# A four-FFN encoder step on one core: loads behind the norm, the convolution's end on VectorE, one tag for each pair of banks

## The chip, the cores and the metric

One core of a Trainium2 chip runs the whole step. The metric is the device time in us, the median of several runs. The profile is one more execution on the same kind of core, recorded by the hardware profiler.

## What is computed

544 tokens (512 of a new stream, 32 that continue a cached one) with 1024 features go through two layers. Each layer is half an FFN, a mixer, and half an FFN; the mixer of the first layer is a convolution module, that of the second is differential attention. Cut to what matters here:

```
x = x + 0.5 * swiglu(rms_norm(x), w_gate, w_up, w_down)      # FFN0
a = rms_norm(x) @ w_pw1 + b_pw1                              # convolution module
u = a[..., :1024] * sigmoid(a[..., 1024:])
c = depthwise_conv(concat(past, u), w_dw, width 31, causal) + b_dw
c = silu(layer_norm(c) * ln_g + ln_b)
x = x + c @ w_pw2 + b_pw2
x = x + 0.5 * swiglu(...)                                    # FFN1
x = x + 0.5 * swiglu(...)                                    # FFN2
x = x + diff_attention(rms_norm(x))
x = x + 0.5 * swiglu(...)                                    # FFN3, then the last norm
```

All of it is float32.

## The kernel before

**Layout.** x lies in eight tiles of 128 features by 544 tokens. A matrix product in float32 is made of three TensorE (PE) products of rounded halves: weight high by data high, high by low, low by high. So every weight stripe (tile wr, ws or wd) is rounded on ScalarE (ACT) into whi (line L313), and the rest wlo is formed on VectorE (DVE) (L123, the helper `two`) before PE may use it; the data have xh and xl likewise. PE works in the tiles pq, py and pd of the FFNs and in a of the convolution, all in PSUM.

**FFNs and loads.** `ffns` opens an FFN and `ffn_body` walks through a plan of jobs; `task(n, f)` puts a piece of work in front of job n. Weights come by SyncE's (SP's) queue through `load(ring)` (L258): ring wr holds whole stripes for gate and up, ws stripes that a GpSimd (POOL) DMA adds others onto (`add_stripe`), wd smaller pieces of both products. `DEPTH` is 3 ws and 5 wd. On entry all of them are loaded (L534; the first FFN has a prologue in its place). Near the first job of the plan that needs the root (g1), `norm` (L667) sums the squares on PE, makes the reciprocal root r, and sends it through DRAM by SP (L484 row, L485 r) so that it is spread over all partitions; right behind it, still in `norm`, it fills the rings that are not full.

**Convolution.** `conv_body` (L754) has eight tiles of u. Four, called D, are convolved on DVE by 31 taps (L794), tap 0 and tap 1 on ACT (L790, L792), with two partial sums added at the end (L801). Four, called PT, are transposed by a trip through DRAM, convolved on PE (`pconv`, L892), written back from PSUM by ACT (L897), and sent out by an ACT DMA (dc, L899) and back by four SP DMAs (c, L902). The layer norm uses a shifted mean: the mean over the first D tile (`shift`, L930), tile mu, is taken from each tile (`center`, L914), the rest squared on ACT (`square`, L919), and both summed on PE (`sums`, L456). `keep_warm` (L467) is a number of matmuls of a constant whose result nobody reads. The statistics (L985 to L989) are broadcast by PE (`quarter_bcast`, L461), copied by ACT (L995), applied on DVE (L1014 to L1018) and ACT (L1021, L1022), and the last matrix product (pw2, `pw2_k`) follows, its lower half made by `y_lo` (L1007), its result added to x by `fin` (L1036).

The order of the work on an engine is the order in which these functions issue it. Eight PSUM banks are used as four pairs that go round, with one tag and four buffers:

```
conv(psum(4, [P, 2, 512], pp, "a", 4), V_F2)
```

Of the kernel before, what the change touches and what calls it, by code (L numbers as in the profile page):

```python
# [12 lines left out]
ALU = mybir.AluOpType  # L13
# [67 lines left out]
def trunk_kernel(ctx, tc, xT, ckT, cv, stT, stP, wtp, vec, gu0, dn0, pw1, pw2, gu1, dn1,  # L81
# [176 lines left out]
    def load(ring):  # L258
        i = nload[ring]
        if i >= (len(rings[ring]) if ring == "wr" else limit[ring]):  # L260
            return
        c = rings[ring][i]
        if ring == "wr":
            c["t"] = wraw.tile([P, WMAX], F32, tag="wr", name="wr")
        else:
            c["t"] = ffn_pool[0].tile([P, WMAX if ring == "ws" else QC], F32, tag=ring, name=ring, bufs=DEPTH[ring])
        nload[ring] += 1
        nc.sync.dma_start(out=c["t"][:, :c["n"]], in_=c["ap"])
        if ring == "ws":
            adding.append((pos["slot"], c))  # L270

    adding = []

# [244 lines left out]
    def product(out, w, off, kind, first, last, ks):  # L518
        hi, lo = w
        for i, k in enumerate(ks):  # L520
            a = off + i * P
            bh, bl = operand(kind, k)
            for z, (wt, b) in enumerate(((hi, bh), (hi, bl), (lo, bh))):
                nc.tensor.matmul(out=out, lhsT=wt[:, a:a + P], rhs=b, start=first and k == 0 and z == 0,  # L524
                                 stop=last and k == 3 and z == 2, skip_group_check=True)

    def ffns(plan, which, prologue=None):

        with tc.tile_pool(name="hp", reuse_waits="tile", bufs=1) as hp, \
             tc.tile_pool(name="pf", reuse_waits="tile", bufs=1, space=bass.MemoryType.PSUM) as pf:  # L530
            ffn_pool[0] = hp
            limit.update(plan["limit"])
            if prologue is None:
                for ring, n in DEPTH.items():  # L534
                    for _ in range(n):
                        load(ring)
            else:
                prologue()
            ffn_body(hp, pf, plan, which, prologue and "start")
            pos["get"] = plan["end"]  # L540

    def ffn_body(hp, pf, plan, which, entry):
# [124 lines left out]
        def norm():  # L667
            norm_a(ptile("y"), [nst["acc"]], AF.Silu)
            norm_c()
            for ring, n in DEPTH.items():  # L670
                while nload[ring] < n:
                    load(ring)

        for f in range(len(which)):
# [6 lines left out]
        for f in range(len(which)):  # L681
            g1 = at["Ga", f, 1, 0]
            start = entry and f == 0
            task(g1 - (1 if f else 0 if start else 2), norm)
            gc = which[f][0]
            sums_at = (-1, 0, 1, 4, 5) if start else (-2, -1, 0, 4, 5) if f else (None, None, None, -3, -2)
            for k, n in enumerate(sums_at):
                if n is not None:
                    task(g1 + n, lambda gc=gc, k=k: quarter_sums(k, gc), True)
            for k in range(KD // 2):  # L690
                task(g1 + (0 if f else 0 if start else 0), lambda k=k: quarter_minus(k), True)
                task(g1 + (3 if f else 3 if start else 3) + k, lambda gc=gc, k=k: quarter_diff(k, gc), True)
# [61 lines left out]
    def conv_body(alloc, next_gc, cp, dp):  # L754
        NO = UE - ST
        WTB = 6
        NFILL = (12, 8)
        WLN = {2: 2, 6: 3}
        taps = []
        u_t, c_t, x_t = {}, {}, {}  # L760
# [18 lines left out]
        def queue_taps(j):  # L779
            e = u_t[j]  # L780
            acc = []

            def tap(t):
                if t == 0:
                    acc.extend((ct(f"c{j}", [P, NO]), ct(f"d{j}", [P, NO])))
                    c_t[j] = acc[0]
                a = acc[t % 2]
                wcol = vcol(V_DW + j * CW + t)
                if t == 0:
                    nc.scalar.activation(out=a, in_=e[:, t:t + NO], func=AF.Identity, scale=wcol, bias=vcol(V_BDW + j))  # L790
                elif t == 1:
                    nc.scalar.activation(out=a, in_=e[:, t:t + NO], func=AF.Copy, scale=wcol)  # L792
                else:
                    nc.vector.scalar_tensor_tensor(out=a, in0=e[:, t:t + NO], scalar=wcol, in1=a,  # L794
                                                   op0=ALU.mult, op1=ALU.add)

            tap(0)
            tap(1)
            for t in range(2, CW):
                taps.append(lambda t=t: tap(t))  # L800
            taps.append(lambda: nc.vector.tensor_tensor(out=acc[0], in0=acc[0], in1=acc[1], op=ALU.add))  # L801

        def segs(j, dst):
            c = c_t[j]
            if j in D_T:
                return [(dst[:, 0:NPR], c[:, 0:NPR]), (dst[:, NPR:T], c[:, NPR + ST:NO])]
            out = []
            for d0, d1, n0, n1 in ((0, NPR, 0, 128), (NPR, T, 136, 144)):
                out.append((dst[:, d0:d1].rearrange("q (n p) -> q n p", p=4),
                            c[:, :, n0:n1].rearrange("q p n -> q n p")))  # L810
            return out

        trips = []
# [69 lines left out]
        def pconv(j):  # L883
            ps = alloc()
            xt = x_t.pop(j)
            cv_sb = ct("cvP", [P, 4, NU], bufs=2)
            b = 4 * P_T.index(j)
            for q in range(4):
                o = ps[:, q % 2, (q // 2) * 256:(q // 2) * 256 + NU]
                w = wt.pop(b + q)  # L890
                for t in range(NJ):
                    nc.tensor.matmul(out=o, lhsT=w[:, t * P:(t + 1) * P], rhs=xt[:, q, t:t + NU],  # L892
                                     start=t == 0, stop=t == NJ - 1)
                wt_load()
            for q in range(4):
                o = ps[:, q % 2, (q // 2) * 256:(q // 2) * 256 + NU]
                nc.scalar.activation(out=cv_sb[:, q, :], in_=o, func=AF.Identity, bias=vcol(V_BDX + 4 * j + q))  # L897
            d = dp.tile([4, 4, 32, NU], F32, tag="dc", name="dc", bufs=2)
            nc.scalar.dma_start(out=d.rearrange("g p c n -> (p c) g n"), in_=cv_sb)  # L899
            c = ct(f"c{j}", [P, 4, NU])  # L900
            for q in range(4):
                nc.sync.dma_start(out=c[32 * q:32 * q + 32], in_=d[q].rearrange("p c n -> c p n"))  # L902
            c_t[j] = c

        dtl = {}
        mu = ct("mu", [P, T])
        nbt = ct("nb", [P, T])

        sq_t = {}

        def center(j, eng):
            t = ct(f"d{j}", [P, T])
            for (o, i_), (m, _) in zip(segs(j, t), segs(j, mu)):
                eng.tensor_tensor(out=o, in0=i_, in1=m, op=ALU.subtract)  # L914
            dtl[j] = t

        def square(j):
# [7 lines left out]
        def shift():  # L925
            pm = alloc()
            c = c_t[D_T[0]]
            for o, src in ((pm[:, 0, 0:HT], c[:, 0:HT]), (pm[:, 1, 0:NPR - HT], c[:, HT:NPR]),
                           (pm[:, 1, NPR - HT:HT], c[:, NPR + ST:NO])):
                nc.tensor.matmul(out=o, lhsT=ones_m, rhs=src, start=True, stop=True)  # L930
            nc.scalar.activation(out=halves(mu), in_=pv(pm), func=AF.Copy)

        def taps_left(n):
            while len(taps) > n * (CW - 1):
# [3 lines left out]
        for j in range(KD):  # L938
# [3 lines left out]
            if j == 4:  # L942

                taps_left(3)
                shift()
                center(D[0], nc.gpsimd)
            elif j == 5:
                square(D[0])
            elif j == 6:
                pconv(PT[0])  # L950
                pop(10)
                taps_left(2)
                center(D[1], nc.gpsimd)
        trips_go()
        nc.scalar.preload_act_table(AF.Sqrt)
        square(D[1])
        pconv(PT[1])
        center(PT[0], nc.gpsimd)
        pop(12)
        pconv(PT[2])  # L960
        square(PT[0])
        pop(10)
        taps_left(1)
        center(D[2], nc.gpsimd)
        center(PT[1], nc.gpsimd)
        pop(4)
        pconv(PT[3])
        square(D[2])
        square(PT[1])
        pop(12)  # L970
        center(PT[2], nc.gpsimd)
        square(PT[2])
        pop(len(taps))
        center(D[3], nc.vector)
        square(D[3])
        pst = alloc()
        for n, j in enumerate((D[0], D[1], PT[0], D[2], PT[1], PT[2])):
            sums(j, n == 0)
        keep_warm(alloc(), NFILL[0])
        sums(D[3])  # L980
        center(PT[3], nc.vector)
        square(PT[3])
        sums(PT[3], last=True)
        rs4, nb4 = ct("rs4", [P, QT]), ct("nb4", [P, QT])
        nc.vector.tensor_copy(out=nb4, in_=pst[:, 0, 0:QT])  # L985
# [17 lines left out]
                mm3(pss[q], w2[0], (k % 2) * 4 + q, yh[k], yl[k], k == 0, k == KD - 1)  # L1003

        def y_lo(j):
            l = ct(f"c{j}", [P, T], F32R)
            nc.vector.tensor_tensor(out=l, in0=dtl[j], in1=f32(yh[j]), op=ALU.subtract)  # L1007
            yl.append(l)

        base = pos["get"]  # L1010
        for j in range(KD):
# [10 lines left out]
            nc.scalar.activation(out=t, in_=t, func=AF.Silu, scale=vcol(V_LNG + j), bias=vcol(V_LNB + j))  # L1022
            yh.append(h)
            if j == 0:
                pss = [alloc() for _ in range(4)]
            elif j in WLN:
                w_ahead(base + WLN[j])
# [13 lines left out]
        for o in range(4):  # L1041
            quarters(o, next_gc)
            flush(1)
            norm_sq(o)
        for o in range(4, KD):
            ps = alloc()
            w = w_get()
            for k in range(KD):
                mm3(ps, w, k, yh[k], yl[k], k == 0, k == KD - 1)
# [406 lines left out]
    with tc.manual_schedule():  # L1456
        nc.scalar.preload_act_table(AF.Sqrt)
        def prologue():
# [25 lines left out]
            for k in range(KD):  # L1484
                nc.sync.dma_start(out=x[k], in_=xT[:, k, :])
                for p in pieces.get(k, ()):
                    part(*p)
            load("wr")
            nc.sync.dma_start(out=vecs[:, V_HEAD:], in_=vec[:, V_HEAD:])
            nc.vector.tensor_scalar(out=ngain, in0=vecs[:, :V_FIN], scalar1=-1.0, scalar2=None, op0=ALU.mult)  # L1490
            for k in range(KD):
# [9 lines left out]
            for c in gates:  # L1501
                used(c)
                used(c)
            load("ws")
            nc.vector.tensor_tensor(out=lprod[:, 0:1], in0=vecs[0:64, V_LAM:V_LAM + 1],
                                    in1=vecs[0:64, V_LAM + 1:V_LAM + 2], op=ALU.mult)
            nc.vector.tensor_tensor(out=lprod[:, 1:2], in0=vecs[0:64, V_LAM + 2:V_LAM + 3],
# [119 lines left out]
```

## Time and profile before

| what | value |
|---|---|
| median of 3 runs | 2007.44 us (2006.48 to 2009.76) |
| the profiled execution | 2004.41 us, its span 2002.6 us |
| PE busy | 1956.4 us (98% of the span), 15548 matmuls |
| DVE, ACT, POOL busy | 1513.2, 977.9, 174.3 us |
| mean granted TensorE clock | 0.992 of full speed |

The rest of the execution's time lies outside the span. The convolution module is from about 400 to 600 us. The busy share of PE by 40 slices of the span (tenths) is 9 almost everywhere and drops in the first slice, in the eleventh (500 to 550 us) and in the last.

### The profile page before, as it was taken

What the parts mean: (1) busy time and instruction counts of PE and PEld (TensorE: products, weight loads), DVE (VectorE), ACT (ScalarE), POOL (GpSimd) and SP (SyncE); (2) the same over time, 40 slices, a digit from 0 to 9 for tenths busy, and PEclk for the clock granted to TensorE, in tenths of its full rate; (3) what the DMA queues carried; (4) which work ended last, traced back from release to release, by engine and by line L of the source; (5) the groups of instructions that cost most, each with busy time, mean ns of one, the idle gap of its engine ahead of it and who ended that gap; (6) DMA issues with size and microseconds to landing.
All of it is one profiled execution on the core that took longest, in us unless ns stands there. A gap on an engine that the chain in (4) does not pass through costs nothing.

```text
span 2002.6 us, 38720 instructions
## 1 busy us (share of the span) xinstructions
PE 1956.4 (98%) x15548; PEld 1922.0 (96%) x15548; DVE 1513.2 (76%) x2724; ACT 977.9 (49%) x1873; POOL 174.3 (9%) x209
## 2 busy tenths in 40 slices
PE   7999999999799999999999999999999999999998
PEld 6999999999699999999999999999888999999997
DVE  7877777699887877777787777776676678777775
ACT  6544444432265544444564444445555555444444
POOL 1000000013401000000000000000111000000000
PEclk9999999999899999999999999999999999999999
DMA  7655553236327655555155555322222256555522
GB/s 210 172 152 144 146 144 102 79 119 200 115 64 194 169 144 142 145 145 156 54 150 160 143 146 144 101 90 88 90 87 86 70 151 173 152 144 146 143 74 71
DMA packets 110787, 260.70 MB, mean 130 GB/s; under 512 B 11752, under 2 KB 23184, under 8 KB 110608
## 3 DMA queue, kind: packets, MB, share of 16 engines
q1 hardware_dynamic: 80528, 204.20, 30.6%
q0 software_dynamic: 25088, 50.69, 14.3%
q10 hardware_dynamic: 4992, 3.34, 0.5%
q8 instruction: 122, 2.00, 0.4%
q14 instruction: 57, 0.47, 0.1%
HBM read 248.87 MB, written 9.31 MB: 129 GB/s over the span
## 4 chain that ended last, share of the span: by engine, by line
PE 61%; DVE 6%; ACT 4%; issue 1%; DMA 1%; POOL 0%; DVEq 0%; ACTq 0%
PE pq L524 27%; PE pd L357 6%; PE pd L363 6%; PE pd L360 6%; PE py L524 4%; PE m L357 2%; PE m L363 2%; PE m L360 2%; DVE wlo L123 1%; ACT e L1167 1%; PE t L1180 1%; PE a L360 1%; PE t L1224 1%; PE a L363 1%; PE a L357 1%
## 5 line engine op out<-in xcount | busy, mean ns | idle before, releaser
L524 PE MATMUL pq<-ar,whi 128*128 128x272 f32 x1920 | 369.2, 289 | 3.2 <-ACT e L579 2.2
L524 PEld LDWEIGHTS pq<-ar,whi 128*128 128x128 f32 x1920 | 302.0, 189 | 4.3 <-ACT e L579 2.7
L123 DVE TENSOR_TENSOR wlo<-wr,whi 128x512 fp32r<-128x512 f32 (+1 forms) x243 | 196.1, 812 | 136.7 <-ACT whi L313 135.5
L524 PE MATMUL pq<-xh,whi 128*128 128x272 f32 x960 | 275.6, 287 | 3.0 <-DVE g L123 3.0
L524 PE MATMUL pq<-ar,wlo 128*128 128x272 f32 x960 | 277.6, 289 | 0.0
L524 PE MATMUL pq<-xh,wlo 128*128 128x272 f32 x960 | 276.5, 288 | 0.0
L524 PE MATMUL pq<-xl,whi 128*128 128x272 f32 x960 | 275.2, 287 | 0.0
L357 PE MATMUL pd<-hh,whi 128*128 128x272 f32 x1224 | 254.9, 289 | 0.2 <-DVE x L663 0.2
L360 PE MATMUL pd<-hl,whi 128*128 128x272 f32 x1224 | 252.8, 288 | 0.0
L363 PE MATMUL pd<-hh,wlo 128*128 128x272 f32 x1224 | 252.6, 288 | 0.0
L313 ACT ACTIVATE whi<-wd 128x512 fp32r<-128x512 f32 (+1 forms) x272 | 162.6, 599 | 162.8 <-issue 126.6
L278 POOL DMA_DIRECT2D ws<-gu x80 | 95.6, 1195 | 1261.8 <-DVE wlo L123 680.3
L123 DVE TENSOR_TENSOR wlo<-wd,whi 128x512 fp32r<-128x512 f32 (+1 forms) x272 | 177.3, 653 | 25.4 <-ACT whi L313 21.2
L357 PEld LDWEIGHTS pd<-hh,whi 128*128 128x128 f32 x1224 | 191.3, 188 | 1.3 <-PE py L363 0.4
L360 PEld LDWEIGHTS pd<-hl,whi 128*128 128x128 f32 x1224 | 192.3, 189 | 0.0
L363 PEld LDWEIGHTS pd<-hh,wlo 128*128 128x128 f32 x1224 | 191.7, 188 | 0.0
L524 PEld LDWEIGHTS pq<-xh,whi 128*128 128x128 f32 x960 | 180.8, 188 | 3.1 <-issue 3.1
L524 PEld LDWEIGHTS pq<-ar,wlo 128*128 128x128 f32 x960 | 181.7, 189 | 0.0
L524 PEld LDWEIGHTS pq<-xl,whi 128*128 128x128 f32 x960 | 180.8, 188 | 0.0
L524 PEld LDWEIGHTS pq<-xh,wlo 128*128 128x128 f32 x960 | 180.5, 188 | 0.1
L313 ACT ACTIVATE whi<-wr 128x512 fp32r<-128x512 f32 (+1 forms) x243 | 173.0, 717 | 15.3 <-PE pq L360 4.4
L663 DVE SCALAR_TENSOR_TENSOR x<-pd,x 128x544 f32<-128x544 f32 x168 | 121.0, 720 | 77.5 <-PE pd L363 77.4
(311 smaller groups left out, 4170.0 us busy)
## 6 DMA issues: line engine op xcount, KB each, us to landing
wr<-gu SPq DMA_DIRECT2D x94, 512.0 KB, 5.0
ws<-gu SPq DMA_DIRECT2D x80, 512.0 KB, 3.4
ws<-gu POOLq DMA_DIRECT2D x80, 512.0 KB, 6.8
wd<-dn SPq DMA_DIRECT2D x160, 256.0 KB, 2.8
wd<-gu SPq DMA_DIRECT2D x80, 256.0 KB, 2.7
wr<-pw SPq DMA_DIRECT2D x24, 512.0 KB, 3.3
wr<-qkv SPq DMA_DIRECT2D x24, 512.0 KB, 3.2
ar<-wtp SPq DMA_DIRECT2D x16, 576.0 KB, 4.8
```

Of the source, the lines that this page charges most:

```text
L123: nc.vector.tensor_tensor(out=out, in0=in0, in1=in1, op=op)
L278: nc.gpsimd.dma_start(out=c["t"].rearrange("p (a c) -> p a c", a=2), in_=c["add"], accum_op=ALU.add)
L313: nc.scalar.activation(out=hi, in_=src, func=AF.Copy)
L357: nc.tensor.matmul(out=o[s], lhsT=wh, rhs=xh[:, s * HT:(s + 1) * HT], start=first, stop=False)
L360: nc.tensor.matmul(out=o[s], lhsT=wh, rhs=xl[:, s * HT:(s + 1) * HT], start=False, stop=False)
L363: nc.tensor.matmul(out=o[s], lhsT=wl, rhs=xh[:, s * HT:(s + 1) * HT], start=False, stop=last)
L524: nc.tensor.matmul(out=out, lhsT=wt[:, a:a + P], rhs=b, start=first and k == 0 and z == 0, stop=last and k == 3 and z == 2, skip_group_che ...
L663: nc.vector.scalar_tensor_tensor(out=out, in0=src, scalar=0.5, in1=out, op0=ALU.mult, op1=ALU.add)
L1167: nc.scalar.activation(out=e[c][:, :n], in_=p, func=AF.Exp, bias=nm[:, c:c + 1], accum_out=sm[:, c:c + 1])
L1180: nc.tensor.matmul(out=p[c][:, :n], lhsT=d[a][pr, qs], rhs=d[b][pr, :n], start=z == 0, stop=z == 2)
L1224: nc.tensor.matmul(out=p[:, q], lhsT=a[:, ks], rhs=b[:, aq], start=(kb == 0 and z == 0), stop=(kb == 3 and z == 2))
```

## The change

**Loads.** An FFN's entry loads 2 ws and no wd; the rest (1 ws, 5 wd) is loaded by a task `fill` at job g1 + 2, behind the norm, in the first FFN of a plan. In the first FFN the two ws are issued before the tail of the constants and the wr of the prologue, where one ws followed the wr before. The DMA adds of ws are at least three jobs apart. **Convolution.** POOL has no centring any more: D0, D1 and the PT tiles are centred on DVE, the third and fourth D tiles have no centre at all, since their tap 1 moves from ACT to DVE and adds mu (held negated), and their closing addition writes 512 and 32 columns together. The PT tiles come back by quarters: four ACT copies each with its own 72 KB DMA out. The order of squares and sums changes, and a third filler group, five matmuls, is put ahead of pw2. **PSUM.** Four tags of one buffer each go round in place of one tag with four, and the last four pw2 rows take theirs ahead of the loop.

```
-            adding.append((pos["slot"], c))
+            adding.append((max(pos["slot"], adding[-1][0] + 3 if adding else 0), c))
...
+    opened = {"ws": 2, "wd": 0}
...
-                for ring, n in DEPTH.items():
+                for ring, n in opened.items():
...
+        def fill():
             for ring, n in DEPTH.items():
-                while nload[ring] < n:
+                while nload[ring] < first[ring] + n - (opened[ring] if not entry or ring == 'ws' else 0):
                     load(ring)
...
             task(g1 - (1 if f else 0 if start else 2), norm)
+            if not f:
+                task(g1 + 2, fill)
...
-        NFILL = (12, 8)
+        NFILL = (12, 8, 5)
...
+            late = j in D_T[2:]
...
+                elif t == 1 and late:
+                    nc.vector.scalar_tensor_tensor(out=a, in0=e[:, t:t + NO], scalar=wcol, in1=mu,
+                                                   op0=ALU.mult, op1=ALU.add)
...
+            def total():
+                c, d = acc
+                if not late:
+                    two(c, c, d, ALU.add)
+                    return
+                two(c[:, :NPR], c[:, :NPR], d[:, :NPR], ALU.add)
+                two(c[:, NPR:T], c[:, NPR + ST:NO], d[:, NPR + ST:NO], ALU.add)
+                dtl[j] = c[:, 0:T]
...
+            def back(q):
+                nc.scalar.activation(out=cv_sb[:, q, :], in_=bank(q), func=AF.Identity, bias=vcol(V_BDX + 4 * j + q))
+                nc.scalar.dma_start(out=d[q].rearrange("p c n -> (p c) n"), in_=cv_sb[:, q, :])
+                nc.sync.dma_start(out=c[32 * q:32 * q + 32], in_=d[q].rearrange("p c n -> c p n"))
...
-            nc.scalar.dma_start(out=d.rearrange("g p c n -> (p c) g n"), in_=cv_sb)
...
-        def center(j, eng):
+        def center(j):
             t = ct(f"d{j}", [P, T])
-            for (o, i_), (m, _) in zip(segs(j, t), segs(j, mu)):
-                eng.tensor_tensor(out=o, in0=i_, in1=m, op=ALU.subtract)
+            for o, i_, m in segs(j, t):
+                two(o, i_, m, ALU.add)
             dtl[j] = t
...
-        for n, j in enumerate((D[0], D[1], PT[0], D[2], PT[1], PT[2])):
+        for n, j in enumerate((D[0], D[1], PT[0], D[2], PT[1])):
             sums(j, n == 0)
         keep_warm(alloc(), NFILL[0])
+        sums(PT[2])
+        pop(len(taps))
+        square(D[3])
+        center(PT[3])
+        square(PT[3])
         sums(D[3])
-        center(PT[3], nc.vector)
-        square(PT[3])
         sums(PT[3], last=True)
...
+                keep_warm(alloc(), NFILL[2])
                 pss = [alloc() for _ in range(4)]
...
+        rows = [alloc() for _ in range(4)]
         for o in range(4, KD):
-            ps = alloc()
+            ps = rows[o - 4]
...
             load("wr")
+            for _ in range(2):
+                load("ws")
...
-            load("ws")
...
-            conv(psum(4, [P, 2, 512], pp, "a", 4), V_F2)
+            each = [psum(4, [P, 2, 512], pp, "a%d" % i, 1) for i in range(4)]
+            conv(lambda: (each.append(each.pop(0)), each[-1]())[1], V_F2)
```

How the order moves, at three places. On SP, behind the norm of the first FFN (row and r are the trip of the norm, wr, ws and wd the rings), first as it stood, then as it stands now:

```order
L484 DMA row<-r_347 4x136
L485 DMA r<-row 128x544
L268 DMA ws<-gu 128x1024 x2
L268 DMA wd<-gu 128x512
L268 DMA wd<-dn 128x256
L268 DMA wd<-gu 128x512
L268 DMA wd<-dn 128x256 x2
L268 DMA wr<-gu 128x1024 x2
```

```order
L484 DMA row<-r_349 4x136
L485 DMA r<-row 128x544
L268 DMA wr<-gu 128x1024 x2
L268 DMA ws<-gu 128x1024
L268 DMA wd<-gu 128x512
L268 DMA wd<-dn 128x256
L268 DMA wd<-gu 128x512
L268 DMA wd<-dn 128x256 x2
```

The two wr have moved in front of the ring's filling, and one ws of it has moved ahead of the row, into the prologue. On DVE, the end of the convolution (c and d the partial sums or centred tiles of a D tile, c_6206 and c_6173 the last PT tile in either program):

```order
L794 SCALAR_TENSOR_TENSOR c_5349<-u_5342,vecs,c_5349 128x574
L801 TENSOR_TENSOR c_5349<-c_5349,d_5350 128x574
L914 TENSOR_TENSOR d_6229<-c_5349,mu 128x512
L914 TENSOR_TENSOR d_6229<-c_5349,mu 128x32
L914 TENSOR_TENSOR d_6304<-c_6206,mu 128x512
L914 TENSOR_TENSOR d_6304<-c_6206,mu 128x32
```

```order
L806 SCALAR_TENSOR_TENSOR c_5349<-u_5342,vecs,c_5349 128x574
L123 TENSOR_TENSOR d_6236<-c_6098,mu 128x512
L123 TENSOR_TENSOR d_6236<-c_6098,mu 128x32
L123 TENSOR_TENSOR c_5349<-c_5349,d_5350 128x512
L123 TENSOR_TENSOR c_5349<-c_5349,d_5350 128x32
L123 TENSOR_TENSOR d_6307<-c_6173,mu 128x512
L123 TENSOR_TENSOR d_6307<-c_6173,mu 128x32
```

The centre of the third PT tile (d_6236) has come to DVE from POOL, and the one of the fourth D tile (d_6229) is gone. On PE, from the sums of the second PT tile to the broadcasts (d and c the centred tiles, u their squares, ones_m alone the fillers):

```order
L456 MATMUL a<-d_6155,ones_d 32x136 x4
L456 MATMUL a<-u_6213,ones_d 32x136 x4
L456 MATMUL a<-d_6224,ones_d 32x136 x4
L456 MATMUL a<-u_6227,ones_d 32x136 x4
L467 MATMUL a<-ones_m 128x128 x12
L456 MATMUL a<-d_6229,ones_d 32x136 x4
L456 MATMUL a<-u_6232,ones_d 32x136 x4
L456 MATMUL a<-d_6304,ones_d 32x136 x4
L456 MATMUL a<-u_6307,ones_d 32x136 x4
L467 MATMUL a<-ones_m 128x128 x8
```

```order
L456 MATMUL a_6241<-d_6163,ones_d 32x136 x4
L456 MATMUL a_6241<-u_6168,ones_d 32x136 x4
L467 MATMUL a_6282<-ones_m 128x128 x12
L456 MATMUL a_6241<-d_6236,ones_d 32x136 x4
L456 MATMUL a_6241<-u_6239,ones_d 32x136 x4
L456 MATMUL a_6241<-c_5349,ones_d 32x136 x4
L456 MATMUL a_6241<-u_6305,ones_d 32x136 x4
L456 MATMUL a_6241<-d_6307,ones_d 32x136 x4
L456 MATMUL a_6241<-u_6310,ones_d 32x136 x4
L467 MATMUL a_6339<-ones_m 128x128 x8
```

The twelve fillers stand one PT tile earlier, so that three pairs of sums follow them in place of two.

## Rows read from the trace of the kernel before

**Rows 1.** Waits of TensorE, whole span: us in total, times, longest us.

```profile
PE a L456 <- POOL d L914: 6.1, 3, 5.1
...
PE py L524 <- DVE g L123: 2.7, 2, 2.1
...
PE pq L357 <- DVE x L1036: 1.5, 1, 1.5
```

**Rows 2.** Windows: window, us, PE busy (x), PEclk, DMA share, GB/s.

```profile
41.00:47.00 6.00, 5.72 (x45) 1.00 0.56 102
...
50.00:54.00 4.00, 4.00 (x20) 0.57 0.09 13
...
541.00:548.00 7.00, 4.13 (x36) 1.00 0.01 2
...
549.00:556.00 7.00, 6.31 (x30) 0.55 0.00 1
```

**Rows 3.** Timeline of SyncE, first FFN: start, us, engine, line, op.

```profile
25.39 2.37 SPq L268 DMA_DIRECT2D ws<-gu  x2
...
30.70 3.33 SPq L268 DMA_DIRECT2D wr<-gu  x2
```

**Rows 4.** Timelines of ScalarE and VectorE, first FFN.

```profile
38.79 0.63 ACT L313 ACTIVATE whi<-wr 128x512 fp32r<-128x512 f32 x1 [3.37 <-DMA wr<-gu]
...
39.45 0.69 DVE L123 TENSOR_TENSOR wlo<-wr,whi 128x512 fp32r<-128x512 f32 x1 [4.08 <-ACT whi L313]
```

**Rows 5.** Timeline of TensorE, first FFN.

```profile
41.28 0.36 PE L524 MATMUL py<-xh,whi 128*128 128x272 f32 x1 [2.06 <-DVE g L123]
...
46.84 0.29 PE L524 MATMUL pq<-ar,wlo 128*128 128x272 f32 x1
...
49.88 0.40 PE L524 MATMUL pq<-ar,whi 128*128 128x272 f32 x1 [1.11 <-ACT e L579]
```

**Rows 6.** Timeline of VectorE, end of the convolution.

```profile
497.11 1.09 DVE L859 SCALAR_TENSOR_TENSOR u<-a,vecs,g 128x512 f32<-128x512 f32 x1
...
509.70 0.80 DVE L794 SCALAR_TENSOR_TENSOR c<-u,vecs,c 128x574 f32<-128x574 f32 x1
...
528.61 0.81 DVE L794 SCALAR_TENSOR_TENSOR c<-u,vecs,c 128x574 f32<-128x574 f32 x1
...
531.43 3.17 DVE L914 TENSOR_TENSOR d<-c,mu 128x512 f32<-128x512 f32 x4
...
556.30 0.72 DVE L1007 TENSOR_TENSOR c<-d,u 128x544 fp32r<-128x544 f32 x1
```

**Rows 7.** Timeline of GpSimd, end of the convolution.

```profile
515.36 19.19 POOL L914 TENSOR_TENSOR d<-c,mu 128x512 f32<-128x512 f32 x4 [5.49 <-DMA c<-dc]
```

**Rows 8.** Timelines of ScalarE and SyncE, end of the convolution.

```profile
524.11 0.37 ACTq L899 DMA_DIRECT2D dc<-cvP  x1
...
526.53 1.73 SPq L902 DMA_DIRECT2D c<-dc  x4
```

**Rows 9.** Timeline of TensorE, end of the convolution.

```profile
535.91 4.05 PE L467 MATMUL a<-ones_m 128*128 128x128 f32 x24
...
540.96 2.05 PE L467 MATMUL a<-ones_m 128*128 128x128 f32 x16
...
544.63 1.09 PE L461 MATMUL a<-nb,selq 128*128 128x136 f32 x8
...
548.06 0.52 PE L357 MATMUL a<-u,whi 128*128 128x272 f32 x2 [2.34 <-ACT u L1021]
...
549.69 0.82 PE L360 MATMUL a<-c,whi 128*128 128x272 f32 x2 [1.11 <-DVE c L1007]
```

**Rows 10.** DMA issues, whole span: xcount, KB each, median us to landing.

```profile
du<-u ACTq DMA_DIRECT2D x16, 72.0 KB, 4.2
...
dc<-cvP ACTq DMA_DIRECT2D x4, 288.0 KB, 6.0
...
c<-dc SPq DMA_DIRECT2D x16, 72.0 KB, 2.0
```

More of the change, by code (lines that the diff above doesn't have):

```diff
@@ L669, in norm @@
             norm_c()
+        first = {ring: nload[ring] for ring in DEPTH}
+        def fill():
             for ring, n in DEPTH.items():
-                while nload[ring] < n:
+                while nload[ring] < first[ring] + n - (opened[ring] if not entry or ring == 'ws' else 0):
                     load(ring)
@@ L795, in tap @@
                                                    op0=ALU.mult, op1=ALU.add)
+            def total():
[6 more added lines that the diff above has]
+                dtl[j] = c[:, 0:T]
             tap(0)
-            tap(1)
-            for t in range(2, CW):
+            if not late:
+                tap(1)
+            for t in range(1 if late else 2, CW):
                 taps.append(lambda t=t: tap(t))
-            taps.append(lambda: nc.vector.tensor_tensor(out=acc[0], in0=acc[0], in1=acc[1], op=ALU.add))
+            taps.append(total)
         def segs(j, dst):
@@ L805, in segs @@
             if j in D_T:
-                return [(dst[:, 0:NPR], c[:, 0:NPR]), (dst[:, NPR:T], c[:, NPR + ST:NO])]
+                return [(dst[:, 0:NPR], c[:, 0:NPR], mu[:, 0:NPR]), (dst[:, NPR:T], c[:, NPR + ST:NO], mu[:, NPR + ST:NO])]
             out = []
-            for d0, d1, n0, n1 in ((0, NPR, 0, 128), (NPR, T, 136, 144)):
+            for d0, d1, n0, n1, m0, m1 in ((0, NPR, 0, 128, 0, NPR), (NPR, T, 136, 144, NPR + ST, NO)):
                 out.append((dst[:, d0:d1].rearrange("q (n p) -> q n p", p=4),
-                            c[:, :, n0:n1].rearrange("q p n -> q n p")))
+                            c[:, :, n0:n1].rearrange("q p n -> q n p"),
+                            mu[:, m0:m1].rearrange("q (n p) -> q n p", p=4)))
             return out
@@ L887, in pconv, with bank @@
             b = 4 * P_T.index(j)
+            d = dp.tile([4, 4, 32, NU], F32, tag="dc", name="dc", bufs=2)
+            c = ct(f"c{j}", [P, 4, NU])
+            def bank(q):
+                return ps[:, q % 2, (q // 2) * 256:(q // 2) * 256 + NU]
+            def back(q):
+                nc.scalar.activation(out=cv_sb[:, q, :], in_=bank(q), func=AF.Identity, bias=vcol(V_BDX + 4 * j + q))
+                nc.scalar.dma_start(out=d[q].rearrange("p c n -> (p c) n"), in_=cv_sb[:, q, :])
+                nc.sync.dma_start(out=c[32 * q:32 * q + 32], in_=d[q].rearrange("p c n -> c p n"))
             for q in range(4):
-                o = ps[:, q % 2, (q // 2) * 256:(q // 2) * 256 + NU]
                 w = wt.pop(b + q)
                 for t in range(NJ):
-                    nc.tensor.matmul(out=o, lhsT=w[:, t * P:(t + 1) * P], rhs=xt[:, q, t:t + NU],
+                    nc.tensor.matmul(out=bank(q), lhsT=w[:, t * P:(t + 1) * P], rhs=xt[:, q, t:t + NU],
                                      start=t == 0, stop=t == NJ - 1)
@@ L895, in pconv @@
             for q in range(4):
-                o = ps[:, q % 2, (q // 2) * 256:(q // 2) * 256 + NU]
-                nc.scalar.activation(out=cv_sb[:, q, :], in_=o, func=AF.Identity, bias=vcol(V_BDX + 4 * j + q))
-            d = dp.tile([4, 4, 32, NU], F32, tag="dc", name="dc", bufs=2)
-            nc.scalar.dma_start(out=d.rearrange("g p c n -> (p c) g n"), in_=cv_sb)
-            c = ct(f"c{j}", [P, 4, NU])
-            for q in range(4):
-                nc.sync.dma_start(out=c[32 * q:32 * q + 32], in_=d[q].rearrange("p c n -> c p n"))
+                back(q)
             c_t[j] = c
         dtl = {}
-        mu = ct("mu", [P, T])
+        mu = ct("mu", [P, NO])
+        nc.gpsimd.memset(mu[:, NPR:NPR + ST], 0.0)
         nbt = ct("nb", [P, T])
         sq_t = {}
-        def center(j, eng):
+        def center(j):
             t = ct(f"d{j}", [P, T])
-            for (o, i_), (m, _) in zip(segs(j, t), segs(j, mu)):
-                eng.tensor_tensor(out=o, in0=i_, in1=m, op=ALU.subtract)
+            for o, i_, m in segs(j, t):
+                two(o, i_, m, ALU.add)
             dtl[j] = t
@@ L930, in shift @@
                 nc.tensor.matmul(out=o, lhsT=ones_m, rhs=src, start=True, stop=True)
-            nc.scalar.activation(out=halves(mu), in_=pv(pm), func=AF.Copy)
+            nc.scalar.activation(out=mu[:, 0:HT], in_=pm[:, 0, :HT], func=AF.Copy, scale=-1.0)
+            nc.scalar.activation(out=mu[:, HT:NPR], in_=pm[:, 1, 0:NPR - HT], func=AF.Copy, scale=-1.0)
+            nc.scalar.activation(out=mu[:, NPR + ST:NO], in_=pm[:, 1, NPR - HT:HT], func=AF.Copy, scale=-1.0)
         def taps_left(n):
@@ L945, in conv_body @@
                 shift()
-                center(D[0], nc.gpsimd)
+                center(D[0])
             elif j == 5:
@@ L952, in conv_body @@
                 taps_left(2)
-                center(D[1], nc.gpsimd)
+                center(D[1])
         trips_go()
@@ L957, in conv_body @@
         pconv(PT[1])
-        center(PT[0], nc.gpsimd)
+        center(PT[0])
         pop(12)
@@ L963, in conv_body @@
         taps_left(1)
[L964 to L967, printed above, removed]
+        center(PT[1])
         square(D[2])
         square(PT[1])
-        pop(12)
-        center(PT[2], nc.gpsimd)
+        pconv(PT[3])
+        pop(14)
+        center(PT[2])
         square(PT[2])
-        pop(len(taps))
-        center(D[3], nc.vector)
-        square(D[3])
         pst = alloc()
-        for n, j in enumerate((D[0], D[1], PT[0], D[2], PT[1], PT[2])):
+        for n, j in enumerate((D[0], D[1], PT[0], D[2], PT[1])):
             sums(j, n == 0)
         keep_warm(alloc(), NFILL[0])
+        sums(PT[2])
[3 more added lines that the diff above has]
+        square(PT[3])
         sums(D[3])
-        center(PT[3], nc.vector)
-        square(PT[3])
         sums(PT[3], last=True)
@@ L1005, in y_lo @@
         def y_lo(j):
-            l = ct(f"c{j}", [P, T], F32R)
+            l = ct(f"d{j}" if j in D_T[2:] else f"c{j}", [P, T], F32R)
             nc.vector.tensor_tensor(out=l, in0=dtl[j], in1=f32(yh[j]), op=ALU.subtract)
```

## The prediction

> **What bounds the kernel now.** I read the waits of the TensorE (PE) over the whole span first, because PE is the engine that hardly rests: an edit can only be worth something where PE stands still or runs at a low clock. Three entries of that view touch the change [rows 1]: 6.1 us for the centred tiles of the convolution (5.1 of it in one piece), 2.7 us in two pieces for VectorE's (DVE's) g at the entry of two FFNs, and 1.5 us for the last residual of the convolution. Then I read the clock that PE was granted, stretch by stretch [rows 2]: 1.00 (2.4 GHz) where PE was busy before, but 0.57 in 50 to 54 us and 0.55 in 549 to 556, which is near the lower of its two levels (1.2 GHz), each time just behind idle time of PE. Last I followed each wait back along the other engines' timelines [rows 3 to 8].
>
> **A. The start of the first FFN (loads).** The second load of the pair of wr stripes that SyncE (SP) issues behind the row r sits behind two ws and five wd loads: the ws are issued from 25.39 us, the wr from 30.70 [rows 3], the pair taking 3.33 us since the second waits. ACT then sits 3.37 us for a wr to land, and DVE 4.08 us for ACT [rows 4]; PE waits 2.06 for the g that is queued on DVE behind that split [rows 5]. The change issues those wr right behind r: 30.70 - 25.39 = 5.3 us earlier, more than the 4.08 us that DVE sits. The g comes forward by more than PE's wait, so A1 = **-2.06 us**. The work behind it (the split of the next stripes, ar, e) costs PE more: at the pitch of 5.72/45 = 0.127 us a matmul [rows 2], the one that starts at 46.84 is followed by five more of the same program order before 49.88 [rows 5]; six take 0.76 of the 3.04 us, and 2.28 are lost. It comes forward by 4.08 at DVE, but PE comes to it 2.06 earlier too, and I estimate that 0.99 of it stays (2.28 less 4.08 - 0.73 - 2.06, where 0.73 is the queue that DVE has to work off anyway, one pass of the size in [rows 4, 6]): A2 = **-1.29**. The clock of 50 to 54 was 0.57; at 1.00 the same columns take 4.00 x 0.43 = 1.7 us less. The wait of 2.06 at 41.28 alone left the clock at 1.00 behind it [rows 2, 5], so with one remaining gap of 1 us I take it as kept: A3 = **-1.7**, bounds 0 and -1.7. A's sum is **-5.05**. What pays: the two ws stripes and the five wd come later by the two wr, and the prologue now puts two ws ahead of the tail of the constants and two wr. No wait of PE in the view names a ws or a wd. The added GpSimd accumulates onto ws are spread by three slots, their number is unchanged. If they and the early ws take the wr's bandwidth by as much as the order gives it, A is 0; that is the other bound.
>
> **B. The end of the convolution.** GpSimd (POOL) stops centring. Before, its last four instructions span 19.19 us after waiting 5.49 for the tap data to come back [rows 7], while DVE works beside them; the four centring instructions that DVE runs there take 3.17 us [rows 6]. After, DVE does everything: u7 at the earliest 0.75 before its start at 497.11, that is 496.36 [rows 6]. From there the new order of DVE is u7, 5 taps, a centre of a tile convolved on PE (PT), 5 taps, the closing addition of the third DVE tile, 16 taps, PT centre, 14 taps, PT centre, closing addition, PT centre. A tap costs (528.61 - 509.70)/26 = 0.727 us [rows 6], a PT centre like u7's strided write 1.09 [rows 6] as the dearer bound, a closing addition 0.81 like a tap's whole time [rows 6]: 5 x 1.09 + 40 x 0.727 + 2 x 0.81 = 36.15, so the last centre ends near 532.5. Before, the last DVE instruction group ended at 531.43 + 3.17 = 534.60 [rows 6], and its sums stood still later: PE had 12 filler matmuls (24 passes) of 4.05 us queued at 535.91 ahead of them, at the low clock, and they ended at 540.96, where the next fillers start [rows 9]. In the new order the fillers come ahead of the sums of the third PT tile, so only a square on ACT (0.6 us, like the pass of [rows 4]) and two short groups of sums, under 1 us, follow the last centre: 534.0. B1 = 534.0 - 540.96 = **-7.0**. Bounds: if all that DVE does takes its bound without any loss and u7 starts early, -7.8; if the last PT tile comes back late, -5.8.
> That trip is the disputed piece. It goes out on ACT's queue and in on SP's. In the middle over the whole span one piece of 288 KB took 6.0 us out, pieces of 72 KB 4.2 on the same queue, and 2.0 each to come in [rows 10]. For this very tile the 288 KB went out at 524.11 and SP could begin to fetch it at 526.53, so it was out in 2.4 us [rows 8]. After, ACT copies and sends by quarters, 0.37 us more a quarter for the issue [rows 8], so the last quarter leaves near 524.11 + 4 x 0.37 = 525.6. With 2.4 and 2.0 it is in at 530.0, and DVE comes to it at 532.5 - 1.1 = 531.4: no wait, B1 stays -7.0. With 4.2 and 2.0 and half of the 1.73 us that SP takes for its four issues [rows 8] it is in at 532.6, 1.2 late: the -5.8. I take the row of this tile itself, since other loads are few there.
> The Trainium skill, DMA: Bandwidth & Descriptors, section Anatomy of one DMA, gives every DMA of the GpSimd path a fixed 2.0 us plus its bytes over a bandwidth, and so speaks against cutting one DMA into four: three more fixed costs. By that figure a quarter out takes an estimated 2.2 us, the last is in near 529.8, and the sum keeps its -7.0, unless the four fixed costs are paid one behind another, which is rival 3. The medians here, 4.2 and 6.0, lie above the page's figure, and by them the sum is -5.8.
> Then PE: the broadcasts ran at clock 1.00, behind 2.05 us of fillers [rows 2, 9]. The new sums come from a PE that has been idle longer, and the broadcasts may run at the low level: they are two of about 1.09 us at full clock [rows 9], so 0 to +2.1; I take B2 = **+0.5**, since most of the fillers that held the clock are still there. Behind the broadcasts PE waits 2.34 us for ACT's first u and 1.11 for DVE's c [rows 9] and then runs 549 to 556 at 0.55. That costs 7.0 x 0.45 = 3.15 us. The change puts five fillers into the first gap. Whether these suffice no row tells: 0 to -3.15; what is late next is DVE's third c, 556.30 + 0.72 = 557.02 [rows 6], which caps it. I take half, B3 = **-1.6**. B's sum is -7.0 + 0.5 - 1.6 = **-8.1**.
>
> **C. PSUM tags.** The first matmul of the FFN behind waits 1.5 us for the last residual [rows 1], because its buffer is the one that this row used. With tags and a filler tile more, the last row sits in another pair of banks and the first matmul asks for a row that was evicted several us earlier: **-1.5**. **D. The entries of the second and fourth FFN.** The r row is issued ahead of one ws and five wd loads; at the fourth, PE waited for g, the smaller of the two pieces, 2.7 - 2.1 = 0.6 to 0.7 [rows 1]: **-0.7**. At the second, the order of r changes under work that PE has anyway, so nothing.
>
> Sum: -5.05 - 8.1 - 1.5 - 0.7 = **-15.4 us**. The profiled execution was 2004.41 us, the median of the runs 2007.44, that is 3.03 above; the change gives 1989.0 in terms of the first and **1992.0** in terms of the second, which is the forecast.
>
> **The rivals.** (1) The start gains nothing: the early ws and the accumulates compete with the wr, which then land no sooner. A = 0, sum -10.3: 1997.1. For it: 5.3 us ahead in the queue is not 5.3 us ahead in landing, and the DMA share of 41 to 47 is still 0.56 [rows 2]. Against: the wr needs to come only 4.08 us earlier, and from 50 on the share is 0.09, so the loads before it are not more than the engines can carry. (2) The end of the convolution gains only part: the quarters make DVE wait (-5.8), the broadcasts run at the low clock (+2.1), and the five fillers don't lift it (0). B = -3.7, sum -11.0: 1996.5. Both together: -5.9, 2001.5. (3) Slower: the quarters out and in queue up behind one another. One trip was 6.0 + 2.0 = 8.0 us and ended where POOL went on at 515.36 [rows 7, 10]. Four in series take 32 us, 24 later: 539.4. DVE now meets that tile itself, in order, at 496.36 + 2 x 1.09 + 26 x 0.727 + 0.81 = 518.3, and all its taps queue behind the waiting centre, where before only POOL stood. It would stand 21.1 us; less the 15.4 won, that is 5.7 us slower: 2013.1. It decides from a slip of 518.3 - 515.36 + 15.4 = 18.3 us on. Against it: the pieces of 72 KB are sent in fours today too, and land in 4.2 us out and 2.0 in [rows 10]. (4) The change does not do what it says: PE's waits have other causes behind the ones named, so that the next of them ends at the same time; about 2007.
>
> **How the numbers follow.** The forecast has 0.58, the start alone failing 0.12, the end alone failing 0.14, both 0.06, no effect 0.06, slower 0.04. A difference of 0.2% (4 us, about what a measurement of this kernel can tell from none) is passed by the first three and by half of the fourth: faster 0.87, same 0.09, slower 0.04. The range goes from the forecast with B1 = -7.8, B2 = 0, B3 = -3.15 (1989.2) and 3 us of the runs' own spread below, 1986, up to both partial cases, 2001.5.
>
> **What would show it.** Right: DVE idles no 4.08 us before 40 us and PE's 2.06 there is gone; the clock of 50 to 54 us is near 1.00; no POOL work at the end of the convolution and no DVE tap over 1 us; the last sums at about 5 + 7 us earlier in the trace than 540.96, near 529 on its own axis; no wait of 1.5 at the hand-over. Wrong: DVE waiting for a quarter in the middle of its taps for over 2 us, a wait for wr, ws or wd in the first 60 us that was not there, or the matmuls behind the broadcasts still at 0.55.

## The result and the profile after

The changed kernel takes 1992.36 us (median of 6 runs, 1990.71 to 1993.75), the kernel before 2006.96 (6 runs, 2003.27 to 2009.76): a ratio of 0.9931, 95% interval 0.9921 to 0.9941, or 13.8 us. The profiled executions are 1992.63 and 2004.41 us, 11.8 apart, since that of before is one of its quicker ones.

The start of the first FFN, changed kernel: TensorE (PE), windows (window, us, PE busy, PEclk, DMA share, GB/s; PEclk is the granted clock as a share of 2.4 GHz), then ScalarE (ACT), GpSimd (POOL), SyncE (SP) and PE in their timelines (start, us).

```profile
35.00:41.00 6.00, 4.53 (x23) 0.56 0.77 211
41.00:47.00 6.00, 6.00 (x50) 1.00 0.20 37
50.00:54.00 4.00, 4.00 (x34) 1.00 0.39 130
```

```profile
26.19 1.16 ACT L313 ACTIVATE whi<-wr 128x512 fp32r<-128x512 f32 x2 [2.04 <-DMA wr<-gu]
...
16.88 2.55 POOL L278 DMA_DIRECT2D ws<-gu  x2 [14.09 <-DMA ws<-gu]
...
27.72 0.33 SPq L485 DMA_DIRECT2D r<-row  x1
28.15 0.89 SPq L268 DMA_DIRECT2D wr<-gu  x2
...
36.47 0.57 PE L524 MATMUL pq<-xh,whi 128*128 128x272 f32 x1 [5.03 <-DVE g L123]
```

The kernel before has a wait of 2.96 at that PE row, and the full clock in 35 to 41 us:

```profile
34.47 0.36 PE L524 MATMUL pq<-xh,whi 128*128 128x272 f32 x1 [2.96 <-DVE g L123]
...
35.00:41.00 6.00, 4.21 (x34) 1.00 1.09 332
```

The wait of 2.06 at 41.28 and the idle time up to 49.88 [rows 5] are gone and 50 to 54 us runs at 1.00 instead of 0.57 [rows 2]. But an earlier wait has grown from 2.96 to 5.03, and the clock is low behind that one (0.56 in 35 to 41).

The end of the convolution, changed kernel, VectorE (DVE) and PE:

```profile
494.95 1.19 DVE L883 SCALAR_TENSOR_TENSOR u<-a,vecs,g 128x512 f32<-128x512 f32 x2
...
529.78 1.20 DVE L123 TENSOR_TENSOR d<-c,mu 128x512 f32<-128x512 f32 x2
```

```profile
524.54 2.94 PE L467 MATMUL a<-ones_m 128*128 128x128 f32 x24
529.11 0.53 PE L456 MATMUL a<-d,ones_d 128*32 128x136 f32 x8 [1.62 <-DVE d L123]
...
532.15 2.05 PE L467 MATMUL a<-ones_m 128*128 128x128 f32 x16
```

Against [rows 9]: the twelve fillers (24 passes) take 2.94 us instead of 4.05 and are over at 527.5, before VectorE's last centre, and the sums end at 532.15 instead of 540.96. From u7 to the end of the last centre VectorE takes 529.78 + 1.20 - 494.95 = 36.03 us; no tap on VectorE is over 0.823 us (those into tile c are shown, those into d have the same maximum):

```profile
L806 DVE SCALAR_TENSOR_TENSOR c<-u,vecs,c x60: 801/808/823, 401.5 to 527.3; 128x574 f32<-128x574 f32 x60
```

### The profile page after: what moved, and what is told of

The parts are those of the page before. It is cut to its first block, busy times and chain, and to the rows that moved or that the text cites. A ratio compares the mean times of both kernels' runs of the same rounds, so it can differ in the third digit from the quotient of the medians.

```text
span 1990.8 us, 38773 instructions
## 1 busy us (share of the span) xinstructions
PE 1952.1 (98%) x15558; PEld 1920.8 (96%) x15558; DVE 1509.8 (76%) x2736; ACT 977.7 (49%) x1873; POOL 147.1 (7%) x198
## 4 chain that ended last, share of the span: by engine, by line
PE 86%; DVE 7%; ACT 4%; DMA 2%; issue 2%; SPq 0%; ACTq 0%; DVEq 0%
PE pq L524 36%; PE pd L357 8%; PE pd L363 8%; PE pd L360 8%; PE py L524 6%; PE a L357 2%; PE a L360 2%; PE a L363 2%; PE m L357 2%; PE m L363 2%; PE m L360 2%; DVE wlo L123 1%; PE pq L357 1%; PE a L926 1%; PE pq L360 1%
```

## The experiments

Every kernel's PE timeline was cut at the same points: the first product of the PT tiles behind the last product of pw1 (the convolution module's first matrix product), the first filler behind the last sums, the first pw2 product with c, and the first product of the next FFN with xl. The first column is the time at the first point, the next three are the stretches between the points, and the rest is from there to the end of the span. Each is one profiled execution; all in us. Every ratio below is to runs of the kernel before taken beside that kernel, whose medians lie between 2006.08 and 2007.96 us.

| kernel | PT products start | to sums' end | to first c | to next FFN | rest |
|---|---|---|---|---|---|
| before | 495.53 | 45.43 | 8.73 | 52.60 | 1400.31 |
| changed | 493.11 | 39.04 | 8.73 | 49.74 | 1400.18 |
| ws behind wr | 491.16 | 38.36 | 8.75 | 49.58 | 1401.15 |
| loads alone | 491.63 | 45.99 | 8.74 | 52.61 | 1399.83 |
| end alone | 497.33 | 39.09 | 8.74 | 51.40 | 1399.64 |
| fillers moved | 497.02 | 42.74 | 8.74 | 52.29 | 1399.81 |
| POOL centres | 493.98 | 40.69 | 8.97 | 49.74 | 1399.42 |
| no third fillers | 491.92 | 38.26 | 8.74 | 49.74 | 1400.54 |
| one dc | 494.28 | 38.38 | 8.74 | 49.57 | 1400.23 |
| rows in loop | 492.84 | 40.19 | 8.74 | 49.59 | 1401.74 |
| changed again | 492.51 | 38.38 | 8.74 | 49.57 | 1401.20 |
| together | 490.76 | 38.14 | 8.74 | 49.70 | 1399.66 |
| adds left out | 491.21 | 38.96 | 8.73 | 49.58 | 1399.32 |

**One part alone: the loads.** The hunks on `adding`, `opened`, `fill` and the prologue, on the kernel before.

> The kernel before with the loads' part alone (two ws and no wd at an entry, the rest behind the norm, the prologue's order, the adds spaced). Theory: it gives what the start of the changed kernel's trace shows, 2.4 us up to the convolution, plus 0.7 at the entry of the fourth FFN: about 3 us faster than before. Rival (the terms A and D of the prediction): 5.05 + 0.7 = 5.7 us faster.

2001.65 us, ratio 0.9976 (0.9964 to 0.9987): 4.8 us, between the two; the interval, 2.6 to 7.2 us, leaves room for both. The theory took the profiled execution of before for a usual one. Two kernels with the old loads (the next two) start the PT products at 497.33 and 497.02, not 495.53.

**One part alone: the convolution's end.** All hunks of `conv_body` but the rows taken ahead.

> The kernel before with the convolution's end alone (centring on VectorE, tap 1 with mu, quarters, order of sums and fillers, the third filler group); loads and PSUM tags as before. Theory: sums that end 6.4 us earlier and a clock that is low for 3 us less behind the broadcasts: 8.0 us faster than before, and 9.5 if the tile that the third filler group takes is what moves the last row to another pair of banks, so that the wait of 1.5 us at the hand-over goes without the tags. Rival (the gain of the end needs the earlier loads of the start): under 5 us.

1998.63 us, ratio 0.9955 (0.9940 to 0.9969): 9.0 us. The rival is out (the interval is 6.2 to 12.0 us). The theory holds, and the trace says in which form: the hand-over's wait stays, in spite of the filler tile (us in total, times, longest):

```profile
PE pq L357 <- DVE x L1058: 1.6, 1, 1.6
```

**The fillers alone**, on the kernel before:

```
-        for n, j in enumerate((D[0], D[1], PT[0], D[2], PT[1], PT[2])):
+        for n, j in enumerate((D[0], D[1], PT[0], D[2], PT[1])):
             sums(j, n == 0)
         keep_warm(alloc(), NFILL[0])
+        sums(PT[2])
```

> The kernel before with one edit: the sums of the third PT tile stand behind the twelve fillers instead of ahead of them. GpSimd still centres. Theory (the larger part of the gain at the convolution's end is that the fillers no longer stand between the last centres and their sums): the last sums end near 536.4 instead of 540.96, 4.5 us faster than before. Rival (GpSimd beside VectorE is what holds the end up): less than 1.5 us faster.

2002.86 us, ratio 0.9982 (0.9973 to 0.9992): 3.6 us (interval 1.6 to 5.4). In the table the sums end 2.7 us sooner, neither 4.5 nor under 1.5. The fillers now wait for GpSimd too, by the sums ahead of them:

```profile
532.37 1.40 PE L456 MATMUL a<-d,ones_d 128*32 128x136 f32 x8 [4.90 <-POOL d L914]
...
534.40 3.90 PE L467 MATMUL a<-ones_m 128*128 128x128 f32 x24
```

So the order alone gives 2.7 of the 45.43 - 39.04 = 6.4 us. The rest comes only with the other edits of the end: no centres on GpSimd, and two centres fewer.

**GpSimd's centres back** in the changed kernel (`center(D[0], nc.gpsimd)` and so on for D0, D1 and three PT tiles).

> The changed kernel with the centres of D0, D1 and the first three PT tiles back on GpSimd; the last PT tile stays on VectorE, D2 and D3 have no centre, order of sums and fillers as changed. Theory (GpSimd beside VectorE stretches both, and its last centre is late): a centre on GpSimd of up to 15 us again, sums that end 2 to 4 us later, so 2 to 4 us slower than the changed kernel (1994.5 to 1996.5). Rival (what was gained beyond the fillers' order is the two centres that are gone, and GpSimd hides the rest): within 1 us of the changed kernel.

Median 2000.6 us, ratio 0.9958 (0.9941 to 0.9975), but the seven runs lie between 1994.34 and 2004.64. That is 8 us above the changed kernel by the medians, 5.4 by the ratios, so the rival falls, and the 2 to 4 us of the theory are too few. The profiled run, 1994.58, is among the quick ones. Its sums end 1.65 us later than in the changed kernel, and PE waits for a GpSimd centre of 9.03 us, where the first centre on GpSimd, at 452.65, takes 2.03. VectorE is stretched too: four taps and a closing addition beside GpSimd's centres take 2.0 to 2.4 us instead of 0.8. So in this execution 4.7 of the 6.4 us stay with GpSimd centring; what makes other runs 6 to 10 us slower its trace doesn't show.

```profile
522.48 9.03 POOL L943 TENSOR_TENSOR d<-c,mu 128x512 f32<-128x512 f32 x2 [6.00 <-DMA c<-dc]
...
530.89 1.33 PE L456 MATMUL a<-d,ones_d 128*32 128x136 f32 x8 [4.92 <-POOL d L943]
...
L806 DVE SCALAR_TENSOR_TENSOR c<-u,vecs,c x60: 802/810/2424, 402.3 to 528.7; 128x574 f32<-128x574 f32 x60
```

**No third fillers** (the `keep_warm(alloc(), NFILL[2])` line out).

> The changed kernel without the third group of fillers (five matmuls behind the broadcasts). Theory (they shorten the stretch of low clock behind the broadcasts): TensorE's gap there is 2.3 us again, the clock stays low until some 6.5 us behind the first product instead of 4.3, 1.6 us slower than the changed kernel. Rival (VectorE's third c sets the pace there, or the fillers do nothing for the clock): within 0.5 us. A second difference is bound up with it: the tile they take is gone, so the last rows sit in another pair of banks and the wait of 1.6 us at the hand-over may be back; the trace tells the two apart.

1993.45 us, ratio 0.9930 (0.9915 to 0.9945). The time can't tell 0.5 from 1.6 us, but the stretch can: 49.74 to the next FFN, as with the fillers. The theory falls. The clock there is low for about 3 us, as in the changed kernel (0.83 and 0.60 in 540 to 543 and 543 to 546), and PE still is not late:

```profile
540.00:543.00 3.00, 3.00 (x16) 0.50 0.00 0
```

The kernel with the rows in the loop (below) has the full clock all through this stretch, and it is 49.59 there:

```profile
543.00:546.00 3.00, 3.00 (x26) 1.00 0.00 0
```

Where PE has the full clock in this stretch it waits for VectorE's third c, as in that kernel (1.10 at 549.16) and in the one with the ws behind the wr:

```profile
545.66 0.52 PE L360 MATMUL a<-d,whi 128*128 128x272 f32 x2 [1.08 <-DVE d L1036]
```

That c is the floor of 49.6 to 49.7 in the table: about 3 us at the low clock cost at most 0.2 us here.

**One transfer out for each PT tile** (`back` only copies; one ACT DMA behind the four).

> The changed kernel with one 288 KB transfer out for each PT tile again instead of four of 72 KB; the four transfers in as they are. Theory (VectorE comes to each centre later than either way of sending brings the tile): within 1 us of the changed kernel; the first centre behind u7 is the only one that could wait. Rival (the quarters are what lets VectorE take the centres without standing): VectorE waits 1 to 2 us at a centre and the sums end that much later.

1993.17 us, ratio 0.9928 (0.9913 to 0.9943). The theory holds: within 1 us of the changed kernel by median and ratio, and VectorE doesn't wait for a tile. The quarters are not what lets VectorE centre.

**The rows in the loop again** (`ps = alloc()` in place of `rows[o - 4]`).

> The changed kernel with the last four rows of pw2 allocated inside their loop again; four tags stay. Theory (the wait at the hand-over to the next FFN hangs on the tags, that is on which pair of banks the next pool's first tile waits for): no wait of 1.6 us comes back, within 0.5 us of the changed kernel. Rival (it hangs on the rows taken ahead): the wait is back, 1.5 us slower.

1993.12 us, ratio 0.9926 (0.9910 to 0.9943), within 1 us of the changed kernel; no hand-over wait. It is gone without the third fillers too, and it stands with the end alone (1.57) and with the loads alone (1.56), so this leaves the tags as its cure. In this trace one quarter did come late, the last. SyncE's fetches of four earlier quarters took 4.28 us (3.10 in the changed kernel), and the ar of the PT products behind them in its queue were issued at 513.24 instead of 511.75; the last quarter went out at 526.25 instead of 524.98. VectorE waited:

```profile
530.71 1.15 DVE L123 TENSOR_TENSOR d<-c,mu 128x512 f32<-128x512 f32 x2 [0.73 <-DMA c<-dc]
```

**The early ws behind the wr** in the changed kernel's prologue:

```
             load("wr")
-            for _ in range(2):
-                load("ws")
...
                 used(c)
                 used(c)
+            for _ in range(2):
+                load("ws")
```

> The change with one edit: the prologue of the first FFN issues its two ws stripes behind its two wr instead of ahead of them. Theory (the two early ws, and the adds onto them that start as soon as they land, take the bandwidth of the wr that ScalarE needs at 24 us): the wait of ScalarE for that wr (2.04 us in the changed kernel, none there before) goes, TensorE's 5.03 us at 36.5 falls back to about 3.0 as before the change, and the clock of 35 to 41 us, 0.56 in the changed kernel, stays at 1.00. That is 2.0 + 0.44 x 4.5 = 4.0 us less than the changed kernel, about 1988.4. Rival (the wr is late for another reason, or the ws are then late where ScalarE first uses one): within 1 us of the changed kernel, with the wait of 5 us still there or a new one behind 42 us.

1990.70 us, ratio 0.9917 (0.9902 to 0.9931), 1.7 us less than the changed kernel by the medians; the intervals overlap, so the trace has to tell. ACT's wait is gone and PE's is 2.96 again (at 34.59); the clock of 35 to 41 is 0.76, not 1.00. The PT products start 1.95 us earlier than in the changed kernel; of the 4.0 foretold, half.

**The adds onto those ws left out**, the loads where the change has them.

> The changed kernel without GpSimd's adds onto the first two ws stripes; the stripes themselves are loaded ahead of the prologue's wr as in the changed kernel. Left out: the two second operands of the first combined weight stripes. Theory (the adds, which start at 16.9 us and move 1 MB while the wr that ScalarE needs at 24 us is under way, are what makes it late): the wait of ScalarE for that wr at 26.2 (2.04 us) goes, and TensorE's wait of 5.03 falls to about 3.0. Rival (the ws loads ahead of it in SyncE's queue make it late): the wait stays at 1 us or more, and TensorE waits 4 to 5 us.

One run, 1989.56 us. The wait at 26.2 is gone (the three roundings from 23.78 on follow without a break), PE's is 2.95, and r leaves at 25.39:

```profile
23.78 1.68 ACT L317 ACTIVATE whi<-wr 128x512 fp32r<-128x512 f32 x3
...
34.66 0.36 PE L528 MATMUL pq<-xh,whi 128*128 128x272 f32 x1 [2.95 <-DVE g L123]
```

The theory holds: it is the adds. The ws loads themselves, ahead in the queue, cost ACT 1.40 us at an earlier wr (19.98; 1.21 in the changed kernel, no wait before), which PE doesn't feel. The DMA share from 17 to 27 us is 0.99 in the changed kernel, 0.36 here, 0.43 in the kernel before:

```profile
17.00:27.00 10.00, 9.52 (x76) 8.73 (x76) 6.43 (x14) 5.71 (x10) 2.43 (x2) 1.00 0.99 215
```

```profile
17.00:27.00 10.00, 9.53 (x76) 8.69 (x75) 8.36 (x18) 7.73 (x14) 0.00 (x0) 1.00 0.36 128
```

(columns: window, us, PE, PEld, DVE, ACT, POOL busy, PEclk, DMA share, GB/s; the changed kernel, then this one).

**The changed kernel again, and three edits together**: ws behind the wr, one dc, `NFILL = (20, 8, 5)`.

> The changed kernel once more, beside the others on one chip, so that they are compared with the same runs of the kernel before. All theories: 1992 to 1993.

> The changed kernel with three edits together: the prologue's two ws behind its two wr, one 288 KB transfer out for each PT tile, and twenty fillers ahead of the last three pairs of sums instead of twelve. Theory: the start gains what the first of them gave (VectorE's g no later than 34.5 us, first product of the PT convolutions near 491.2), the sums end at most 38.3 us behind that, the rest as before: 1989 to 1990.5, faster than the changed kernel by 2 to 3 us. Rival (the differences between these kernels are what the runs scatter by): 1991.5 to 1993.5, the same as the changed kernel.

1992.12 us (1991.34 to 1994.95) and 1989.72 us (1988.74 to 1990.51), ratios 0.9936 (0.9923 to 0.9948) and 0.9921 (0.9908 to 0.9935): the runs don't overlap, so the rival falls. The joined kernel is 2.4 us ahead of the change by the medians. The two profiled executions are 3.4 apart: 1.75 from the start (490.76 against 492.51), 0.1 from the convolution's end, and 1.5 from the rest, which no edit touched. That the other two edits add anything to the ws behind the wr (1989.42 to 1991.35) isn't shown.

## Why the prediction was right, and where it was not

Forecast 1992.0, measured 1992.36. Step by step:

**A, forecast -5.05; -2.4 in the profiled pair.** The step "The change issues those wr right behind r: 30.70 - 25.39 = 5.3 us earlier" failed in size. They left at 28.15, 2.55 us earlier than 30.70 [rows 3]: r itself left at 27.72 instead of 25.00, as its row took longer on full DMA queues (share 0.99 in 17 to 27 us). That alone cost nothing that the trace shows, since ACT no longer waits for those wr. What cost time is what the sum put at nothing: the two early ws and the adds onto them. ACT stood 2.04 us for a wr that the prologue had loaded, and the first g came 2.0 us later (VectorE begins it at 35.89 instead of 33.89). That is all of A1: 2.96 + 2.06 of PE's waits became 5.03. The text held this case as the bound "A is 0" and as rival 1, and its own sign of being wrong, a wait for a wr that was not there, did come. The truth lies between, because A2 and the clock behind it (A3) did come. The clock was then low earlier, 0.56 in 35 to 41; the longer wait is not its whole reason, since with PE's wait back at 2.96 and 2.95 it was still 0.76 (ws behind the wr) and 0.72 (adds left out).
By the profiled pair A is 495.53 - 493.11 = -2.4. Over three traces with the old loads (mean 496.6) and seven with the change's (mean 492.9) it is -3.7; with the ws behind the wr, -5.7 (two traces, mean 491.0), and with the adds left out the PT products start at 491.21.

**B1, -7.0: right.** 6.4 in the profiled pair; means of 38.7 (eight traces with the new end, two of them with one transfer out) against 45.7 (two with the old) give 7.0. VectorE's path of 36.15 us was 36.03. The start of u7 that was taken 0.75 us early came 1.84 behind the first PT product, against 1.58 before, so that allowance was not there; the sums behind the last centre were 0.3 us shorter than taken. What the 7.0 is made of is told apart only in part: 2.7 by the order alone, and with GpSimd's centres back 1.65 is lost in the one execution that was profiled, more in others. What the two missing centres give by themselves no run shows.
The dispute over quarters was empty: the 72 KB took 3.7 us in the middle, between the 4.2 of [rows 10] and the 2.2 estimated from the Trainium skill, DMA: Bandwidth & Descriptors, section Anatomy of one DMA. That page gives its figure for the GpSimd path, and these transfers go out by ScalarE's queue, so the estimate was a loan from another path, and the measured 3.7 decides. One transfer did as well as four, and rival 3 is excluded: no quarter kept VectorE waiting for more than 0.73 us in any trace.

**B2, +0.5: 0.** 8.73 before and after.

**B3, -1.6: the size nearly right, the reason not.** Less the wait of 1.54 at the hand-over, the stretch went from 51.06 to 49.74, -1.3. But without the third fillers it is the same 49.74, so they are not what gives it. What shortens the low clock there when the end before it is the new one was not found; what ends the gain is VectorE's third c, as the text said. The half that was taken came near by luck.

**C, -1.5: right**, by the tags, and not by the filler tile that the text named beside them.

**D, -0.7: not to be told.** The wait at the last FFN's entry (0.68 at 1647.43) is gone in the changed kernel. But a wait for g of 0.94 stands at 988.43, at the third FFN, where the kernel before has none; the changed kernel again has 0.24 there, and the loads alone none. The rest of the span scatters by 2.4 us in the table (1399.3 to 1401.7). The wait at the last FFN was 0.43 in the kernel with the end alone, which has the old loads, and absent in the one with the fillers moved, which has them too.

The sum by these means is -3.7 - 7.0 - 1.3 - 1.5 = -13.5, against 13.8 measured by the ratio and -15.4 forecast. That the forecast lies only 0.4 us from the median is in part luck. A gave 1.4 less than its sum and D can't be seen, but the median of before came out 0.5 lower in six runs than in three, and by the medians the change is 14.6. The sum also took its terms from a profiled execution of before whose start was 1.1 us better than the mean of three.

## What to carry to other kernels

A load moved forward brings what hangs on its landing forward too. Here the early stripes in the queue cost PE nothing, but the transfers that start when they land filled the DMA engines while a more urgent stripe and a small round trip were under way. Fillers that are to keep a clock up are better placed ahead of work that is still being made than between finished work and its last step: here that order alone was worth 2.7 us of 6.4.

## What was not expected

The same code's start scatters: with the old loads the wait for g at 41 us was 2.06 in one execution, 3.8 in another (the kernel with the end alone) and 3.4 in a third (fillers moved). One profile is therefore a poor yardstick for a term of 2 us; the place in the program, compared over several traces, was a better one. With GpSimd's centres put back into the changed kernel its seven runs scatter over 10 us; those of the kernel before, where GpSimd centres too, over 5 to 6.5, and those of the kernels with all centres on VectorE over 2 to 6. The cause stays open.
